# Operand addresses modulo 64 in the dense products, the timing of residual rows, and the buffers of the closing steps of a streaming-encoder block

## The chip, the cores and the metric

The kernel runs on one core of one Trainium2 chip. The time is the device time of one execution in microseconds (us), from launch to end. The profile and the trace come from one further execution of the same program, whose own time and whose span (first to last instruction) are given below.

The engines are named as in the profile: PE is the matrix engine (TensorE) and PEld its loading of the stationary operand, DVE the vector engine, ACT the scalar engine, POOL GpSimd, and SP the engine that issues most DMAs. SPq, ACTq and POOL rows of kind DMA_DIRECT2D are DMA issues on those engines' queues.

## The reference, cut to what matters

One layer over 2048 rows of 1024 numbers, all float32:

```python
h = rms_norm(x, pre_mix_g);  proj = h @ w_in          # 1024 x 5376
y_a = chunk_band_attention(...);  y_b = rwkv7_time_mix(...)
merged = gate_a * (y_a @ proj_a) + gate_b * (y_b @ proj_b)
x = x + rms_norm(merged @ w_out, post_mix_g)
hf = rms_norm(x, pre_ffn_g)
u = square(relu(hf @ w_up)) @ w_down                  # 1024 x 4096, 4096 x 1024
x = x + rms_norm(u, post_ffn_g)
```

## The kernel before

**Dense products.** Each float32 product is made of three fp32r matmuls: every operand is split into a high part (a cast on ACT, line 76) and a low part (a subtraction on DVE, line 77), and `mm3` (line 85) multiplies high by high, high by low and low by high. In the profile a matmul is named out<-moving,stationary: `ps_u<-t3h,s3l` streams 512 columns of `t3h` past a 128 x 128 block of `s3l`.

**Stages.** The 2048 rows are four groups of 512. For each group the *mixing* runs: `w_in` (psd), time mixing, attention, gates (ps_p) and `w_out` (ps_o). Then come the two *halves* of the feed-forward part, two groups each: `phase_up` (tile `ps_u`) and `phase_down` (tile `ps_dn`). Both use Strassen's scheme: seven block products in place of eight. In `phase_up`, block column i (of 16) needs the products A11, A12 (moving operands `bh`, `bl`), S2, S3, S1, S4 and A22 (moving `t2`, `t3`, `t1`, `b22`, `t4`), 12 matmuls each. The products A11 and A12 of the first eight columns are made ahead, and A11 is kept in tile `z`. In `phase_down` a `product` is 4 row tiles of 12 matmuls, seven products for each of three batches, with plain products of four blocks of `w_down` ahead of and behind them.

**Where tiles lie.** Pools grow from both ends of the on-chip memory. On the left stand `const` (ident 512 bytes a partition, g2c 32, nhalf 32), then in mixing the pools of weights and `h`, and in the feed-forward part `z` (which `phase_down` uses for its stationary tiles `fop`), the first half's `b` tiles (`bh`, `bl`, and `fop2` in `phase_down`), and the tiles t1 to t4, b22 and y. On the right stand, in mixing, `mconst` (with `carry`) and the time mixing's tiles, and in the feed-forward part the raw weights, the stationary tiles of `phase_up` (a1, s12, s3, s4), and the second half's `b` tiles.

**Residual rows.** The sums x + rms_norm(merged @ w_out) of groups 2 and 3 (eight row tiles of 128) are made inside the first half's `phase_up`, by the generator `residuals` (line 1070 on). Each `advance(beside, 1)` between two block products runs it to its next `yield`. A row tile takes seven steps: load o and x; squares of o; scale, add and store x1; squares of x; scaled copy (line 1102); two steps of four transposes (line 1110), copies with the gain (line 1112) and a store. Its o and x live in slices 2, 3 and 4, 5 of `z`, and the gain in slices 0, 1. From column HELD = 6 on, each of the last five block products is followed by a step, and from column 8 on the first two share one more.

**Closing steps.** `phase_down` ends with eight row tiles of two halves (n = 0, 1) of 512 columns: the last matmuls are added to y (line 1373), `halve` squares y on ACT (line 1436) and multiplies y by the gain in place on DVE (line 1437), and `final` sums the squares and makes the root on POOL (lines 1443, 130, 132), then multiplies and adds x on DVE (line 1448) and stores from y (line 1449): on POOL's queue in the first half, on SP's and ACT's in the second. `final` of a row tile stands behind the first addition of the next one. Its x row (`x1r`, two buffers) is loaded inside `final`.

**Order.** A tile scheduler orders each engine's instructions from the code's order and its dependencies; `issue_after(ins)` keeps instructions behind `ins` on the same engine. Each engine and each DMA queue runs in that order.

Of the kernel before, what the change touches and what calls it, by code (L numbers as in the profile page):

```python
# [17 lines left out]
P = 128  # L18
# [14 lines left out]
FIRST, BATCHES, XB = 2, 3, 4  # L33
HELD = 6
PARTS = ("a11", "a12", "a22", "s1", "s2", "s3", "s4")
# [18 lines left out]
class Block:  # L54
# [102 lines left out]
    def constants(self, ctx, mixing):  # L157
# [5 lines left out]
        make_identity(nc, self.ident)  # L163
        self.g2c = keep.tile([P, KB], F32, name="g2c")
        self.nhalf = keep.tile([P, 8], F32, name="nhalf")
# [30 lines left out]

        self.carry = cp.tile([P, 14], F32, name="carry")
        nc.vector.memset(self.carry, 0.0)
# [874 lines left out]
    def residuals(self, z, mp, cb, pt):  # L1073
# [13 lines left out]
        for g in range(2, self.NG):  # L1087
            for t in range(GT):
                ts = slice(t * P, (t + 1) * P)
                nc.sync.dma_start(o, self.od[g][t])  # L1090
                nc.sync.dma_start(x, a["x"][g * G + t * P : g * G + (t + 1) * P])
                yield
                r = lengths(o, 0.25 / D, 0.5)
                yield
                with tc.issue_after(self.add):
                    nc.vector.scalar_tensor_tensor(o, o, r, gp, op0=ALU.mult, op1=ALU.mult)
                    nc.vector.tensor_tensor(x, x, o, ALU.add)
                nc.gpsimd.dma_start(self.x1[g][ts], x)
                yield
                r = lengths(x, 1.0 / D, None)  # L1100
                yield
                nc.scalar.activation(o, x, AF.Copy, scale=r)
                yield
                for h in range(2):
                    ps = pt.tile([P, 4, P], F32, tag="tr", name="ps_ht")
                    f = cb.tile([P, 4, P], F32, tag="c", name="hf")
                    with tc.issue_after(self.mm):
                        for j in range(4):
                            k = h * 4 + j
                            nc.tensor.transpose(ps[:, j], o[:, k * P : (k + 1) * P], self.ident)  # L1110
# [81 lines left out]
    def phase_up(self, half, zp, rp, cb, pn, sp, early, made, beside_of=None):  # L1192
# [7 lines left out]
        with ExitStack() as ctx:  # L1200
# [40 lines left out]
            def hidden(src, x, fb, th, out=None):  # L1241
# [4 lines left out]
                self.add = nc.vector.tensor_tensor(out, src, x, ALU.add).ins  # L1246
                nc.scalar.activation(out, out, AF.Relu)
                nc.scalar.activation(out, out, AF.Square)
# [23 lines left out]
            for i in range(FF // P // 2):  # L1272
# [18 lines left out]
                if i < early:  # L1291
                    p1 = z[:, i]
                    if summed(i):
                        nc.sync.dma_start(R["a11"], place(i, "a11"))
                else:
                    p1 = up.tile([P, G], F32, tag="p1", name="p1")
                    nc.scalar.copy(p1, product(A11, B11, self.pd, "d"))
                    hidden(p1, product(A12, B21, self.pd, "d"), 2 * i, 0, out.get("a11"))
                    advance(beside, 1)
# [17 lines left out]
    def phase_down(self, half, zp, bp, rp, cb, pn, follow=None):  # L1317
# [12 lines left out]
        with ExitStack() as ctx:  # L1330
# [100 lines left out]

            def halve(th, t, n, gt, ssq):
# [3 lines left out]
                nc.scalar.activation(sq, u, AF.Square, accum_out=ssq[:, n : n + 1])  # L1436
                nc.vector.tensor_tensor(u, u, gt[:, ns], ALU.mult)  # L1437

            def final(th, t, fp, ssq):
# [3 lines left out]
                nc.gpsimd.tensor_tensor(ssq[:, 0:1], ssq[:, 0:1], ssq[:, 1:2], ALU.add)  # L1443
# [53 lines left out]
            for th in range(2):  # L1497
                for t in range(GT):
                    ssq = fp.tile([P, 2], F32, tag="ssq", bufs=4, name="ssqu")
                    for n in range(2):  # L1500
# [12 lines left out]
                        halve(th, t, n, gt, ssq)  # L1513
                    done = th, t, fp, ssq
            final(*done)
# [3 lines left out]
    def run(self):  # L1519
        tc, e = self.tc, None  # L1520
        with ExitStack() as ctx, ExitStack() as mixing:
# [47 lines left out]
            with ExitStack() as c:  # L1569
                bp = bpool(c, "b")  # L1570
                advance(self.first_half(0, bp))
                with self.nc.allow_non_contiguous_dma(reason="one vector"):
                    self.nc.gpsimd.dma_start(self.g2c, self.a["pre_ffn_g"].rearrange("(k p) -> p k", p=P))
                with ExitStack() as u:
# [53 lines left out]
```

## Time and profile before

| | us |
|---|---|
| median of three runs (lowest, highest) | 3335.2 (3334.75, 3336.52) |
| the profiled execution | 3334.86 |
| its span | 3333.2 |
| mixing (four groups), 0 to 2021.3 of the span | 2021.3 |
| first half up / down, to 2359.3 / 2679.5 | 338.0 / 320.2 |
| second half up / down, to 2998.8 / 3333.2 | 319.3 / 334.4 |

The stages are cut at the first matmul of each. A row of the timeline gives start, busy time, engine, line, operation, tiles and count; in brackets the engine's idle time before it and what ended it. Rows with a count merge instructions that follow each other, so their busy time runs from the first start to the last end. A row of the waits gives who waited for whom, the sum in us, how often, and the longest.

### The profile page before, as it was taken

Reading aid. Unit: us, or ns where it says so; the run is one execution under the profiler, and the core shown is the slowest. Engines: PE = TensorE matmul, PEld = TensorE weight load, DVE = VectorE, ACT = ScalarE, POOL = GpSimd, SP = SyncE. Lnnn points to the kernel's source line nnn. Section 1 sums busy time; section 2 is a strip of 40 time slices with the busy share of each in tenths; the row PEclk is TensorE's granted clock in tenths of the full one; section 3 lists DMA queues with packets and bytes.
Section 4 is the critical chain, followed back from the end, with each engine's and each line's share of the span. In section 5 each row is a group of like instructions: output and inputs, shape, how many; then the busy total and the mean of one; then the engine's idle time right before and its main releaser. Section 6 shows DMA issues by size and latency. Waiting matters only on the chain. (4 is left out here: it accounts for less than half of the span.)

```text
span 3333.2 us, 49202 instructions
## 1 busy us (share of the span) xinstructions
PE 3236.2 (97%) x18945; PEld 2578.1 (77%) x18945; DVE 2271.5 (68%) x3782; ACT 1571.5 (47%) x2551; POOL 386.6 (12%) x757
## 2 busy tenths in 40 slices
PE   7999999999999999999999999999999999999998
PEld 6877787877777877778777777778788877887887
DVE  6784557765566765666775665777678978776687
ACT  4535534445644444645444635466443454454332
POOL 2110011101021011021111000133000111100001
PEclk9999999999999999999999999999999999999999
DMA  5224343225273234273224266566455564543443
GB/s 157 90 89 148 106 143 108 73 93 179 89 244 120 64 105 169 84 240 127 77 96 154 72 230 215 191 235 229 175 189 202 177 225 168 169 164 134 158 151 126
DMA packets 165874, 497.29 MB, mean 149 GB/s; under 512 B 18108, under 2 KB 26496, under 8 KB 160264
## 3 DMA queue, kind: packets, MB, share of 16 engines
q1 hardware_dynamic: 106740, 357.78, 32.5%
q0 software_dynamic: 22688, 77.61, 6.1%
q10 hardware_dynamic: 36212, 58.76, 4.8%
q8 instruction: 149, 2.44, 0.3%
q14 instruction: 85, 0.70, 0.1%
HBM read 365.08 MB, written 132.15 MB: 149 GB/s over the span
## 5 line engine op out<-in xcount | busy, mean ns | idle before, releaser
L85 PE MATMUL psd<-hh,whi 128*128 128x512 f32 x1344 | 542.0, 403 | 6.1 <-ACT whi L76 3.9
L85 PE MATMUL psd<-hl,whi 128*128 128x512 f32 x1344 | 534.8, 398 | 0.4 <-DVE hl L154 0.4
L85 PE MATMUL psd<-hh,wlo 128*128 128x512 f32 x1344 | 535.1, 398 | 0.0
L85 PE MATMUL ps_dn<-fop,fop 128*128 128x512 f32 x2016 | 464.5, 392 | 1.4 <-DVE y L1373 1.0
L76 ACT CAST whi<-wraw 128x1024 fp32r<-128x1024 f32 x232 | 243.3, 1049 | 460.7 <-PE psd L85 326.7
L85 PEld LDWEIGHTS ps_dn<-fop,fop 128*128 128x128 f32 x2016 | 378.2, 188 | 87.4 <-issue 2.1
L77 DVE TENSOR_TENSOR wlo<-wraw,whi 128x1024 fp32r<-128x1024 f32 x232 | 282.8, 1219 | 143.3 <-ACT whi L76 128.4
L85 PEld LDWEIGHTS psd<-hh,whi 128*128 128x128 f32 x1344 | 253.4, 189 | 62.6 <-ACT whi L76 4.6
L85 PEld LDWEIGHTS psd<-hh,wlo 128*128 128x128 f32 x1344 | 253.7, 189 | 56.0 <-issue 3.5
L85 PEld LDWEIGHTS psd<-hl,whi 128*128 128x128 f32 x1344 | 254.2, 189 | 48.9 <-issue 2.2
L76 ACT CAST fop<-ar 128x1024 fp32r<-128x1024 f32 x84 | 87.8, 1050 | 221.6 <-PE ps_dn L85 177.3
L85 PE MATMUL ps_dn<-fop 128*128 128x512 f32 x768 | 178.5, 393 | 1.6 <-DVE y L1373 1.2
L85 PEld LDWEIGHTS ps_dn<-fop 128*128 128x128 f32 x768 | 143.5, 188 | 36.0 <-DVE y L1373 3.1
L1373 DVE TENSOR_TENSOR y<-y,ps_dn 128x512 f32<-128x512 f32 x168 | 110.6, 685 | 50.2 <-PE ps_dn L85 49.9
L77 DVE TENSOR_TENSOR fop<-ar,fop 128x1024 fp32r<-128x1024 f32 x84 | 102.4, 1222 | 44.2 <-ACT fop L76 44.2
L904 DVE CUSTOM_DVE_ANT_0 sc<-bias,ps_s 128x640 f32<-128x640 f32 (+4 forms) x128 | 94.2, 736 | 51.6 <-PE ps_s L898 49.0
L909 ACT ACTIVATE sc<-sc,mn 128x640 f32<-128x640 f32 (+4 forms) x128 | 97.7, 763 | 35.4 <-DVE mn L904 30.9
L1029 PE MATMUL ps_o<-wlo,mh 128*128 128x512 f32 x256 | 103.1, 403 | 5.7 <-DVE wlo L77 5.7
L1029 PE MATMUL ps_o<-whi,ml 128*128 128x512 f32 x256 | 102.5, 400 | 0.0
L85 PE MATMUL ps_p<-yh,whi 128*128 128x512 f32 x256 | 101.1, 395 | 1.3 <-DVE th L995 1.3
L85 PE MATMUL ps_p<-yh,wlo 128*128 128x512 f32 x256 | 101.5, 396 | 0.2 <-DVE wlo L77 0.2
L1029 PE MATMUL ps_o<-whi,mh 128*128 128x512 f32 x256 | 101.6, 400 | 0.0
(384 smaller groups left out, 6819.2 us busy)
## 6 DMA issues: line engine op xcount, KB each, us to landing
wraw<-in_w_in_dram SPq DMA_DIRECT2D x168, 512.0 KB, 3.7
ar<-sd SPq DMA_DIRECT2D x42, 1024.0 KB, 4.6
wraw<-in_w_up_dram SPq DMA_DIRECT2D x80, 512.0 KB, 4.9
sd<-slots POOLq DMA_DIRECT2D x96, 256.0 KB, 5.2
qb<-in_w_down_dram SPq DMA_DIRECT2D x24, 1024.0 KB, 7.5
gd<-gate ACTq DMA_DIRECT2D x64, 256.0 KB, 3.4
wraw<-in_w_out_dram SPq DMA_DIRECT2D x32, 512.0 KB, 3.7
sd<-slots ACTq DMA_DIRECT2D x60, 256.0 KB, 4.5
```

The source lines that it names most:

```text
L76: self.nc.scalar.copy(hi, src)
L77: self.nc.vector.tensor_tensor(lo, src, hi.bitcast(F32), ALU.subtract)
L85: mm = nc.tensor.matmul(ps, l, r, start=start and n == 0, stop=stop and n == last).ins
L904: nc.vector.tensor_tensor_reduce(sc[:, 0:n], bias[:, s0:640], pss[:, c0 : c0 + n], 1.0, 3.0e38, ALU.add, ALU.min, mn,)
L909: nc.scalar.activation(sc[:, 0:n], sc[:, 0:n], AF.Exp, scale=-1.0, bias=mn, accum_out=sm)
L1029: nc.tensor.matmul(ps[t], l[:, k, ts], r[:, k % 2], start=k == 0 and j == 0, stop=k == KB - 1 and j == 2)
L1373: self.add = nc.vector.tensor_tensor(dst, dst, ps, ALU.add).ins
```

## The change

The change has three parts. No instruction is added or removed on PE, DVE, ACT, POOL or a DMA queue; waits, places and addresses change.

1. **Addresses.** g2c is allocated with 64 bytes instead of 32 and carry with 88 instead of 56, so everything behind g2c on the left, and everything inside of carry on the right during mixing, moves by 32 bytes. Start addresses modulo 64 in the built program:

| product | moving, stationary before | after |
|---|---|---|
| psd, ps_p, ps_o (mixing) | 0, 0 | 32, 32 |
| ps_u with t1 to t4, b22 (both halves) | 0, 32 | 32, 32 |
| ps_u with bh, bl: first half / second half | 0, 32 / 32, 32 | 32, 32 / 32, 32 |
| ps_dn, seven products: first half / second half | 0, 0 / 32, 0 | 32, 32 / 32, 32 |
| ident with left tiles / with the time mixing's tiles (transposes) | 0, 0 / 0, 32 | 0, 32 / 0, 0 |
| small products of the time mixing's low-rank weights (64 matmuls) | 32, 32 | 0, 32 |

2. **Residual rows.** HELD is 5; a row tile takes nine steps: o is loaded a step ahead of x, and a step is put between the scaled copy and the transposes. Squares and copy stand behind the latest relu of the products on ACT (`self.act`). Column 5 gets steps, and columns from 8 on get one more.
3. **Closing steps.** The product with the gain goes to a new tile `scaled` (two buffers); x has four buffers, is loaded at the start of its row tile's step, takes the sum, and is stored from.

```diff
-HELD = 6
+HELD = 5
-        self.g2c = keep.tile([P, KB], F32, name="g2c")
+        self.g2c = keep.tile([P, 2 * KB], F32, name="g2c")
-        self.carry = cp.tile([P, 14], F32, name="carry")
+        self.carry = cp.tile([P, 22], F32, name="carry")
...
                 nc.sync.dma_start(o, self.od[g][t])
+                yield
                 nc.sync.dma_start(x, a["x"][g * G + t * P : g * G + (t + 1) * P])
                 yield
-                r = lengths(o, 0.25 / D, 0.5)
+                with tc.issue_after(self.act):
+                    r = lengths(o, 0.25 / D, 0.5)
...
-                r = lengths(x, 1.0 / D, None)
+                with tc.issue_after(self.act):
+                    r = lengths(x, 1.0 / D, None)
                 yield
-                nc.scalar.activation(o, x, AF.Copy, scale=r)
+                with tc.issue_after(self.act):
+                    nc.scalar.activation(o, x, AF.Copy, scale=r)
+                yield
                 yield
...
-                nc.scalar.activation(out, out, AF.Relu)
+                self.act = nc.scalar.activation(out, out, AF.Relu).ins
...
                     nc.scalar.copy(p1, product(A11, B11, self.pd, "d"))
+                    advance(beside, 1)
                     hidden(p1, product(A12, B21, self.pd, "d"), 2 * i, 0, out.get("a11"))
...
-                nc.vector.tensor_tensor(u, u, gt[:, ns], ALU.mult)
+                nc.vector.tensor_tensor(scaled[:, ns], u, gt[:, ns], ALU.mult)
...
-                x = fp.tile([P, D], F32, tag="x", name="x1r")
-                nc.sync.dma_start(x, self.x1[gs[th]][t * P : (t + 1) * P])
...
-                    u = y[th][:, t, ns]
-                    nc.vector.scalar_tensor_tensor(u, u, r, x[:, ns], op0=ALU.mult, op1=ALU.add)
-                    queue.dma_start(self.out[row : row + P, ns], u)
+                    nc.vector.scalar_tensor_tensor(
+                        x[:, ns], scaled[:, ns], r, x[:, ns], op0=ALU.mult, op1=ALU.add
+                    )
+                    queue.dma_start(self.out[row : row + P, ns], x[:, ns])
...
                 for t in range(GT):
+                    scaled = fp.tile([P, D], F32, tag="scaled", name="scaled")
+                    x = fp.tile([P, D], F32, tag="x", bufs=4, name="x1r")
+                    nc.sync.dma_start(x, self.x1[gs[th]][t * P : (t + 1) * P])
```

What the change moves is shown at two places. The first is SP, from the closing steps of the first half to the start of the second half's `phase_up`: x1r are the x rows, wraw the raw weights of `phase_up`, bl and t2l operands of the second half. Before:

```order
L1171 DMA bl<-ht_338 128x1024 x3
L1442 DMA x1r<-x_0_316 128x1024
L1178 DMA wraw<-in_w_up_dram 128x1024 x3
L1442 DMA x1r<-x_0_316 128x1024
L1178 DMA wraw<-in_w_up_dram 128x1024
L1442 DMA x1r<-x_1_317 128x1024 x4
L1178 DMA wraw<-in_w_up_dram 128x1024 x2
L1219 DMA t2l<-td_373 128x1024 x2
L1219 DMA t3l<-td_373 128x1024 x2
```

The same place on SP after the change:

```order
L1506 DMA x1r<-x_1_317 128x1024
L1176 DMA bl<-ht_338 128x1024
L1183 DMA wraw<-in_w_up_dram 128x1024 x2
L1506 DMA x1r<-x_1_317 128x1024
L1183 DMA wraw<-in_w_up_dram 128x1024 x2
L1506 DMA x1r<-x_1_317 128x1024 x2
L1183 DMA wraw<-in_w_up_dram 128x1024
L1224 DMA t2l<-td_373 128x1024 x2
L1224 DMA t3l<-td_373 128x1024 x2
```

One load of raw weights instead of two now stands between the last x row and t2l, and the four loads of x rows in a row are spread.

The second place is DVE in the second half's closing steps, one row tile and the start of the next. Before:

```order
L1448 SCALAR_TENSOR_TENSOR y_26897<-y_26897,rs_r,x1r 128x512 x2
L1437 TENSOR_TENSOR y_26898<-y_26898,g_post_28785 128x512
L1373 TENSOR_TENSOR y_26898<-y_26898,ps_dn 128x512
L1437 TENSOR_TENSOR y_26898<-y_26898,g_post_28785 128x512
L1373 TENSOR_TENSOR y_26898<-y_26898,ps_dn 128x512
```

The same place on DVE after the change:

```order
L1451 SCALAR_TENSOR_TENSOR x1r<-scaled,rs_r,x1r 128x512 x2
L1443 TENSOR_TENSOR scaled<-y_26906,g_post_28793 128x512
L1379 TENSOR_TENSOR y_26906<-y_26906,ps_dn 128x512
L1443 TENSOR_TENSOR scaled<-y_26906,g_post_28793 128x512
L1379 TENSOR_TENSOR y_26906<-y_26906,ps_dn 128x512
```

The order is the same; the product with the gain no longer overwrites what ACT squares, so it no longer waits for ACT.

More of the change, by code (lines that the diff above doesn't have):

```diff
@@ L1430, in add, with halve @@
                 nc.vector.tensor_tensor(o[:, t], o[:, t], x[:, t], ALU.add)
-            def halve(th, t, n, gt, ssq):
+            def halve(th, t, n, gt, scaled, ssq):
                 ns = slice(n * H, (n + 1) * H)
@@ L1436, in halve, with final @@
                 nc.scalar.activation(sq, u, AF.Square, accum_out=ssq[:, n : n + 1])
-                nc.vector.tensor_tensor(u, u, gt[:, ns], ALU.mult)
-            def final(th, t, fp, ssq):
+                nc.vector.tensor_tensor(scaled[:, ns], u, gt[:, ns], ALU.mult)
+            def final(th, t, fp, scaled, x, ssq):
                 row = gs[th] * G + t * P
-                x = fp.tile([P, D], F32, tag="x", name="x1r")
-                nc.sync.dma_start(x, self.x1[gs[th]][t * P : (t + 1) * P])
                 nc.gpsimd.tensor_tensor(ssq[:, 0:1], ssq[:, 0:1], ssq[:, 1:2], ALU.add)
@@ L1512, in phase_down @@
                             advance(beside, 1)
-                        halve(th, t, n, gt, ssq)
-                    done = th, t, fp, ssq
+                        halve(th, t, n, gt, scaled, ssq)
+                    done = th, t, fp, scaled, x, ssq
             final(*done)
@@ L1572, in run @@
                 with self.nc.allow_non_contiguous_dma(reason="one vector"):
-                    self.nc.gpsimd.dma_start(self.g2c, self.a["pre_ffn_g"].rearrange("(k p) -> p k", p=P))
+                    self.nc.gpsimd.dma_start(self.g2c[:, 0:KB], self.a["pre_ffn_g"].rearrange("(k p) -> p k", p=P))
                 with ExitStack() as u:
```

## The prediction

> **What bounds the kernel.** I read the page first, then the stages cut at their first matmul, then the starts of PE's matmuls in the timeline.
>
> ```profile
> span 3333.2 us, 49202 instructions
> PE 3236.2 (97%) x18945; PEld 2578.1 (77%) x18945; DVE 2271.5 (68%) x3782; ACT 1571.5 (47%) x2551; POOL 386.6 (12%) x757
> ```
>
> PE is busy for 97%. So there are two ways to gain: its matmuls come closer together, or the few waits between them go. The stages, with the busy time (count) of PE, PEld, DVE, ACT and POOL, the granted clock, the DMA share and GB/s; first the mixing, then first half up and down, second half up and down, and last a stretch ahead of the final closing steps:
>
> ```profile
> 0.00:2021.30 2021.30, 1953.94 (x13410) 1543.98 (x13411) 1292.04 (x2545) 964.17 (x1649) 253.13 (x513) 0.99 0.38 128
> 2021.30:2359.30 338.00, 327.11 (x1410) 260.73 (x1409) 240.99 (x318) 201.65 (x359) 69.20 (x128) 0.98 0.63 219
> 2359.30:2679.50 320.20, 317.64 (x1394) 260.78 (x1393) 258.80 (x312) 124.88 (x161) 20.91 (x34) 1.00 0.53 186
> 2679.50:2998.80 319.30, 313.02 (x1346) 252.06 (x1345) 231.45 (x312) 160.13 (x226) 31.89 (x58) 1.00 0.52 181
> 2998.80:3333.20 334.40, 324.47 (x1393) 260.52 (x1391) 248.20 (x297) 120.66 (x160) 11.46 (x24) 0.99 0.41 143
> 3257.00:3288.00 31.00, 31.00 (x135) 24.88 (x134) 28.95 (x38) 11.74 (x12) 0.00 (x0) 1.00 0.29 102
> ```
>
> The two halves do the same products with different times, and in opposite ways: up takes 338.0 and 319.3 us, down 320.2 and 334.4. The count of matmuls is nearly the same and the clock is 1.00 in two of the four, 0.98 and 0.99 in the others. The timeline of PE (start, busy time, line, tiles, count) shows more:
>
> ```profile
> 2404.29 75.87 PE L85 MATMUL ps_dn<-fop,fop 128*128 128x512 f32 x334
> 3099.74 80.43 PE L85 MATMUL ps_dn<-fop,fop 128*128 128x512 f32 x344
> ...
> 2026.87 0.40 PE L85 MATMUL ps_u<-bh,s12h 128*128 128x512 f32 x1
> ...
> 2032.47 0.40 PE L85 MATMUL ps_u<-bh,s3h 128*128 128x512 f32 x1
> ...
> 2843.01 0.40 PE L85 MATMUL ps_u<-bh,a1h 128*128 128x512 f32 x1
> ...
> 2848.46 0.40 PE L85 MATMUL ps_u<-t2h,s12h 128*128 128x512 f32 x1
> ...
> 2851.26 0.40 PE L85 MATMUL ps_u<-t3h,s3h 128*128 128x512 f32 x1
> ```
>
> The last matmul of a run is busy for about 0.4 us, so starts lie (75.87 − 0.39)/333 = 226.7 ns apart in the first half's down stage, where both operands start at 0 modulo 64, and (80.43 − 0.40)/343 = 233.3 ns in the second half's, where they are at 32 and 0. In up it is the reverse: 24 starts from bh,s12h at 2026.87 to bh,s3h at 2032.47 (0 and 32) are 233.3 ns each; 24 from 2843.01 to 2848.46 in the second half (32 and 32) are 227.1; and the 12 that follow at once, with t2 (0 and 32), are 233.3 again. The price follows the agreement of the two addresses through one stretch of one stage, and not the stage or the clock.
>
> **Part 1, addresses.** How many matmuls change from disagreeing to agreeing:
>
> ```profile
> L85 PE MATMUL ps_u<-t3h,s3l 128*128 128x512 f32 x128 | 52.1, 407 | 3.4 <-DVE s3l L77 3.4
> L85 PE MATMUL ps_u<-bh,a1h 128*128 128x512 f32 x176 | 69.5, 395 | 2.8 <-ACT z L1267 2.8
> L85 PE MATMUL ps_u<-bh,s12h 128*128 128x512 f32 x48 | 19.1, 397 | 1.8 <-ACT z L1267 1.5 <-DVE r L1246 0.3
> L85 PE MATMUL ps_u<-bh,s3h 128*128 128x512 f32 x32 | 12.6, 392 | 0.0
> L85 PE MATMUL ps_dn<-fop,fop 128*128 128x512 f32 x2016 | 464.5, 392 | 1.4 <-DVE y L1373 1.0 <-DVE v L1373 0.3
> L916 PE MATMUL ps_pt<-ident,sc 128*128 128x128 f32 x560 | 85.5, 279 | 2.0 <-ACT VV L857 1.2 <-DVE sc L912 0.8
> L516 PE MATMUL ps_bk<-ident,BK 128*128 128x128 f32 x128 | 21.6, 281 | 0.0
> ```
>
> Five products with t1 to t4 and b22, three matmul groups of 128 each: 1920, in both halves. The products with bh and bl, 3 × (176 + 48 + 32) = 768, of which the first half's 384 change. Of the 2016 in down, the second half's 1008. Together 3312. Between the rows above the difference is 233.3 − 227.1 = 6.2 ns or 233.3 − 226.7 = 6.6. At 6.2, which is from neighbouring products of one stage, that is 20.5 us (at 6.6 21.9): 8.3 in the first half's up (1344), 6.0 in the second's (960), 6.2 in the second's down.
>
> Three deductions. The 64 small products that lose their agreement cost 64 × 6.2 ns = 0.4. In the 31 us ahead of the last closing steps DVE is busy for 28.95, 93%, so PE cannot run ahead of it: its 135 matmuls give back 0.8. And where PE waits for a split (the row of s3l below), a faster PE waits longer; two columns of 84 matmuls so lose 2 × 84 × 6.2 ns = 1.0. **A = 20.5 − 2.2 = 18.3 us.** The 5568 matmuls of psd, ps_p and ps_o go from 0, 0 to 32, 32 and still agree: nothing. If it were the 0 that counts they would be dear; that is a rival below. The transposes I put at nothing: those of sc agree with ident before and take 279 ns, those of BK don't and take 281. The largest group, 560, loses its agreement: between nothing and 560 × 2 ns = 1.1 us, which the 128 of BK give back in part.
>
> One rule of the Trainium skill speaks against this term. Its page "TensorE: Matmul & The Clock Gate", section "Step-by-step: what each phase is for", says that PE has two independent SBUF read ports and that loading the next weights "doesn't steal SBUF read bandwidth from the running matmul". By it A would be nothing and the sum 3320; the rows at 2843 to 2851 disagree with it, 227.1 against 233.3 ns.
>
> **Part 2, residual rows.** The waits of the columns with residual rows, 2170 to 2360 (who waited for whom: sum, times, longest), one row tile in the timeline, and the granted clock behind the longest of these waits:
>
> ```profile
> PEld ps_ht L1110 <- ACT z L1102: 8.2, 5, 2.6
> PE ps_ht L1110 <- ACT z L1102: 5.6, 4, 1.9
> PEld ps_u L85 <- DVE s3l L77: 2.2, 1, 2.2
> ...
> 2193.98 0.63 ACT L1082 ACTIVATE sqo<-z 128x512 f32<-128x512 f32 x1 [0.70 <-DVE z L1097]
> ...
> 2198.12 0.63 ACT L1247 ACTIVATE slots<-slots 128x512 f32<-128x512 f32 x1 [2.80 <-DVE slots L1246]
> ...
> 2200.03 1.15 ACT L1102 ACTIVATE z<-z,rs_r 128x1024 f32<-128x1024 f32 x1 [0.61 <-POOL rs_r L132]
> 2201.24 1.09 PE L1110 MATMUL ps_ht<-ident,z 128*128 128x128 f32 x8 [1.09 <-ACT z L1102]
> ...
> 2348.00:2353.00 5.00, 4.35 (x16) 3.65 (x17) 2.36 (x2) 4.46 (x8) 0.85 (x1) 0.66 0.60 222
> ```
>
> The row tile's squares, relu, copy and transposes stand in the middle. From the squares of x (2193.98) to the end of the scaled copy (2201.18) it takes 7.2 us; the code gives it two steps of 12 matmuls, 2 × 2.8 = 5.6, so PE arrives first and waits. With the additional step it has three, 36 × 0.227 = 8.2, and the wait goes with 1.0 to spare. PE lost between 5.6 (its own row) and 8.2 us (that of PEld, under which the previous matmul still runs), middle 6.9. The clock behind the longest wait is 0.66 for 5 us, so its 4.35 busy us would have taken (at 1.00) about 4.35 × 0.66 = 2.9: 1.5 more. **B = 6.9 + 1.5 = 8.4.**
>
> What it adds: column 5 gets steps, DVE work of a row tile that lay elsewhere before, and the order "behind the relu" on ACT. In the row at 2198.12 the relu itself comes 2.80 late from DVE; squares that stand behind such a relu start up to 2.8 late, and behind them POOL's sum and the copy. Over 1.0 spare that leaves at most 1.8 for a row tile. The next waits are on s3l (2.2) and on the transposes' results. B lies between 3 and 11 (8.2 + 1.5, and half of s3l's wait if the spread of steps frees DVE).
>
> **Part 3, closing steps.** The end of the second half:
>
> ```profile
> 3290.64 0.19 POOL L1443 TENSOR_TENSOR ssqu<-ssqu 128x1 f32<-128x1 f32 x1 [324.88 <-ACT squ L1436]
> ...
> 3308.67 15.03 PE L85 MATMUL ps_dn<-fop 128*128 128x512 f32 x64
> ...
> 3319.96 0.68 DVE L1373 TENSOR_TENSOR y<-y,ps_dn 128x512 f32<-128x512 f32 x1
> ...
> 3321.49 0.69 DVE L1437 TENSOR_TENSOR y<-y,g_post 128x512 f32<-128x512 f32 x1 [0.85 <-ACT squ L1436]
> 3321.54 0.70 POOL L1443 TENSOR_TENSOR ssqu<-ssqu 128x1 f32<-128x1 f32 x1 [3.54 <-ACT squ L1436]
> ...
> 3325.11 0.68 DVE L1373 TENSOR_TENSOR y<-y,ps_dn 128x512 f32<-128x512 f32 x1
> ```
>
> PE ends at 3323.70, but the last sum on DVE starts at 3325.11, 1.4 us later. DVE's chain over a row tile has a period of 3325.11 − 3319.96 = 5.15, and in it the product with the gain (line 1437) waits 0.85 for ACT's squares and then starts together with POOL's sum, which takes 0.70 in its company and 0.19 alone (the row at 3290.64). With its own output tile the product starts behind the addition; POOL's sum is then 0.5 shorter and the period about 4.65, under PE's 24 × 0.227 = 5.45. So DVE keeps up and the lag of 1.4 goes, as do 0.5 from the final chain: **C1 = 1.9** (0.5 to 2). If the product met another POOL instruction instead, 0.5 would stay. The x rows and stores cost nothing here: four buffers of x come round after 4 × 5.15 = 20.6 us.
>
> Between the halves, in the waits of 2680 to 2735 and the timeline of SP and ACT:
>
> ```profile
> PEld ps_u L85 <- ACT z L1267: 5.2, 2, 3.2
> ...
> 2681.16 10.23 SPq L1178 DMA_DIRECT2D wraw<-in_w_up_dram  x2
> 2691.69 0.87 SPq L1219 DMA_DIRECT2D t2l<-td  x2
> ...
> 2697.09 1.05 ACT L1162 CAST t2h<-t2l 128x1024 fp32r<-128x1024 f32 x1 [1.99 <-DMA t2l<-td]
> ```
>
> The first products of the second half wait 5.2 us for copies on ACT (z), which stand behind the closing steps' squares and the cast of t2. t2l comes late: its load is issued at 2691.69, behind two loads of raw weights that held SP's queue for 10.23, and its memory is that of y, which the stores of the closing steps still read. After the change one load of weights stands ahead of it, stores read x, and DVE's chain is shorter by the 0.85 and 0.5 of above. The waits could go whole (5.2, with some 1.5 more ahead of them) or stay whole, if t2l's load is held by its data's own late write. I take **C2 = 4.5** (0 to 6.7), nearer to the upper end since both of its causes are moved.
>
> **Sum.** 18.3 + 8.4 + 1.9 + 4.5 = 33.1 us. Against the profiled execution, 3334.86 − 33.1 = 3301.8; the median of the runs, 3335.2, is 0.3 above it. Forecast 3302, chance 0.80; its own range from the terms' ends is 3295 (A 21.9 − 2.2, B 11, C 2 + 6.7) to 3313 (A 18.3, B 3, C 0.5).
>
> **Rivals.** *DVE and ACT pace the up stages* (0.11). DVE is busy for 241 of 338.0 us in the first half's up, 71%, ACT for 60%, and the load is uneven. If half of the 14.3 us of both up stages is given back in longer waits for splits (7), and half of B (4), the time is 3302 + 11 = 3313. Against it: PE's idle time in these stages is only 11 and 6 us.
>
> *The change of addresses does nothing* (0.05): the 6.6 ns belong to something else that changes from half to half. In every disagreeing pair of these rows one tile lies on the left and one on the right, so "the other end of the memory" would explain the rows as well. Then A is 0: 3301.8 + 18.3 = 3320. Against it: by the addresses of the built program, in the first half t1 lies at 144 to 158 KB and s12 at 181 to 185, close by, and its starts are 233 ns apart; in the second half b lies at 169 to 199 KB and a1 at 141 to 145, as far, with 227. If B and C came to less than 8 of their 14.8 as well, the time would be within 0.2% of before.
>
> *Slower: the 0 counts, and not the agreement* (0.04). If a tile at 32 costs the price whatever the other is, the mixing's 5568 matmuls go from free to dear: 5568 × 6.6 ns = 36.7, and A is 0: 3320 + 37 = 3357. It decides against the change from 14.8/5568 = 2.7 ns a matmul on. Against it stands the row pair at 2843.01 and 2848.46: 32 and 32, 227.1 ns.
>
> **Chances and range.** About 0.2%, 6.7 us, is what a measurement of this kernel can tell from no change. Faster by more: forecast 0.80, DVE and ACT 0.11, and 0.02 of "nothing", 0.93; within: 0.03; slower: 0.04. The range 3294 to 3316 holds the forecast's own range, a microsecond for the transposes at its lower end, and the first rival, whose share beyond 3313 reaches some 3 further.
>
> **What would show it.** Starts 227 ns apart in all four stages of the halves, and mixing still 2021 us long (2058 by the slower rival). No wait of ps_ht on z over 1 us, and no clock of 0.66 behind it. POOL's sum at 0.19 in the closing steps, and the last addition within 0.3 us of PE's last matmul. The wait on z at the second half's start below 2 us, with t2l's load issued some 5 us sooner behind PE's first matmul of the stage or ahead of it. Wrong would be: 233 ns anywhere in the halves, or waits for splits in the up stages that grow by more than 3 us together.

## The result, and the profile after

The changed kernel takes 3311.0 us (median of four runs, 3308.97 to 3313.13) against 3335.0 before. The ratio is 0.9932 with a 95% interval of 0.9915 to 0.9949: it is faster by 22.7 us (17 to 28). A second set of runs, beside other kernels, gave 0.9935 (0.9922 to 0.9948). The forecast was 3302 and the range 3294 to 3316. So the direction and the size are right, and about 10 us of the forecast 33 are missing. By stage, in the profiled executions:

| stage | before | after | forecast for the stage | measured |
|---|---|---|---|---|
| mixing | 2021.3 | 2016.3 | 0 | −5.0 |
| first half up | 338.0 | 326.0 | −16.7 (addresses 8.3, residual rows 8.4) | −12.0 |
| first half down | 320.2 | 330.3 | 0 | +10.1 |
| second half up | 319.3 | 313.1 | −10.5 (addresses 6.0, start 4.5) | −6.2 |
| second half down | 334.4 | 325.7 | −8.1 (addresses 6.2, end 1.9) | −8.7 |

The forecasts by stage are those of the terms before the small deductions. Of the mixing's 5 us some 0.8 belong to the change: 384 of the products ps_p go from 229.1 to 226.9 ns, as shown below. The rest is open. Three profiles with the mixing of before have 2018.1 to 2021.3 us, mean 2020.1, and eight with the changed one 2013.5 to 2019.7, mean 2016.3, so that the two overlap. The first row to look at is the third: a stage in which nothing was to happen is 10 us longer. These are the windows of the changed kernel, with the columns as before:

```profile
0.00:2016.30 2016.30, 1950.36 (x13410) 1541.11 (x13411) 1292.07 (x2545) 964.89 (x1649) 252.32 (x513) 1.00 0.38 128
2016.30:2342.30 326.00, 315.80 (x1409) 258.99 (x1408) 239.94 (x317) 195.95 (x347) 65.73 (x126) 0.99 0.65 227
2342.30:2672.60 330.30, 320.08 (x1396) 262.55 (x1395) 258.62 (x310) 129.65 (x171) 17.72 (x35) 0.99 0.51 182
2672.60:2985.70 313.10, 307.76 (x1346) 253.01 (x1345) 231.54 (x315) 159.29 (x226) 31.62 (x60) 0.99 0.53 183
2985.70:3311.40 325.70, 317.19 (x1393) 260.67 (x1391) 247.91 (x297) 121.18 (x160) 7.62 (x24) 0.99 0.41 146
```

In the first half's down stage (third row) the granted clock is 0.99 where it was 1.00, and ACT does 129.65 us of work where it did 124.88: five us of ACT's work came over from the stage before. The timeline of PE and one group of matmuls show the addresses:

```profile
2403.69 26.68 PE L85 MATMUL ps_dn<-fop,fop 128*128 128x512 f32 x117
...
3098.73 41.64 PE L85 MATMUL ps_dn<-fop,fop 128*128 128x512 f32 x183
...
L85 PE MATMUL ps_u<-t3h,s3l 128*128 128x512 f32 x128 | 50.1, 391 | 1.9 <-DVE s3l L77 1.9
```

In the second half's down stage starts are now (41.64 − 0.39)/182 = 226.6 ns apart, as in the first half's ((26.68 − 0.39)/116 = 226.6); before they were 233.3. The mean of t3h,s3l fell from 407 to 391 ns.

Next, the waits of the columns with residual rows (2130 to 2342 us), and ACT, PE and the windows at the seam of the first half's two stages:

```profile
PEld ps_ht L1115 <- ACT z L1106: 8.3, 5, 2.1
PE ps_ht L1115 <- ACT z L1106: 6.1, 5, 1.7
...
2341.45 1.09 PE L1115 MATMUL ps_ht<-ident,z 128*128 128x128 f32 x8 [1.66 <-ACT z L1106]
...
2345.83 0.63 ACT L1117 ACTIVATE hf<-ps_ht,g2c 128x128 f32<-128x128 f32 x2
2350.89 1.14 ACT L1117 ACTIVATE hf<-ps_ht,g2c 128x128 f32<-128x128 f32 x4 [4.43 <-DMA ad<-r]
2351.90 1.58 ACT L1377 COPY y<-ps_dn 128x512 f32<-128x512 f32 x3
...
2352.56 6.68 PE L85 MATMUL ps_dn<-fop 128*128 128x512 f32 x18 [7.26 <-ACT y L1377]
...
2352.00:2358.00 6.00, 5.44 (x14) 4.29 (x15) 0.00 (x0) 4.34 (x9) 0.75 (x1) 0.54 1.04 413
```

Read from below: PE stands still for 7.26 us at the start of down, waiting for ACT's copies of the first sums (y<-ps_dn), and then runs at a granted clock of 0.54. ACT is late with these copies because it stands at 2346.5 to 2350.9 in front of the last four copies with the gain (hf). These want a buffer which they share with the tiles r, and by the profile the store of such a tile (ad<-r, issued on ACT's queue between 2341.9 and 2345.5) is still under way. The last row tile's eight transposes (2341.45) are now the last work of the up stage. Before, its two groups of four stood 10.6 and 6.0 us ahead of the first matmul of down:

```profile
2348.65 1.11 PE L1110 MATMUL ps_ht<-ident,z 128*128 128x128 f32 x4 [1.92 <-ACT z L1102]
...
2353.21 0.60 PE L1110 MATMUL ps_ht<-ident,z 128*128 128x128 f32 x4
...
2359.24 1.09 PE L85 MATMUL ps_dn<-fop 128*128 128x512 f32 x4
```

And the waits of transposes on the scaled copy, which were to go, are as before: 8.3 us (PEld) and 6.1 (PE) against 8.2 and 5.6.

At the start of the second half, the waits of PE in the first 55 us and SP's load of t2l:

```profile
PEld ps_u L85 <- ACT z L1272: 2.8, 1, 2.8
...
2675.38 0.91 SPq L1224 DMA_DIRECT2D t2l<-td  x2
2679.29 0.63 ACT L1442 ACTIVATE squ<-y 128x512 f32<-128x512 f32 x1 [2.00 <-DVE y L1379]
```

One wait of 2.8 is left of two with 5.2 together. t2l is loaded 2.8 us behind the stage's first matmul and no longer 12.2. The closing steps of the second half:

```profile
3289.80 13.99 PE L85 MATMUL ps_dn<-fop 128*128 128x512 f32 x61
...
3303.82 0.69 DVE L1379 TENSOR_TENSOR y<-y,ps_dn 128x512 f32<-128x512 f32 x1
3304.54 0.69 DVE L1443 TENSOR_TENSOR scaled<-y,g_post 128x512 f32<-128x512 f32 x1
3305.40 0.19 POOL L1447 TENSOR_TENSOR ssqu<-ssqu 128x1 f32<-128x1 f32 x1 [4.33 <-ACT squ L1442]
```

PE ends at 3303.79 and the last sum starts at 3303.82, where it was 1.4 us late. The product with the gain no longer waits, and POOL's sum takes 0.19.

### The profile page after: what moved, and what is told of

Read it like the earlier page. It is cut to its first block, busy times and chain, and to the rows that moved or that the text cites. A ratio compares the mean times of both kernels' runs of the same rounds, so it can differ in the third digit from the quotient of the medians.

```text
span 3311.4 us, 49181 instructions
## 1 busy us (share of the span) xinstructions
PE 3211.2 (97%) x18945; PEld 2576.3 (78%) x18945; DVE 2270.1 (69%) x3782; ACT 1571.0 (47%) x2551; POOL 375.0 (11%) x757
## 5 line engine op out<-in xcount | busy, mean ns | idle before, releaser
L85 PE MATMUL ps_dn<-fop,fop 128*128 128x512 f32 x2016 | 457.8, 389 | 1.7 <-DVE y L1379 1.3
```

Source lines behind the costliest of these rows:

```text
L85: mm = nc.tensor.matmul(ps, l, r, start=start and n == 0, stop=stop and n == last).ins
```

## The experiments

Each kernel was timed beside the kernel before on the same chip. Runs of one kernel spread widely (the 23 runs of the kernel before in the first set lie between 3326.0 and 3342.0), so ratios are given with intervals, and the stages of a profile say where a difference lies.

| run | ratio (95% interval) | us against before |
|---|---|---|
| e1 addresses | 0.9958 (0.9942 to 0.9974) | −14.0 |
| e2 residual rows | 1.0004 (0.9994 to 1.0014) | +1.3 |
| e3 closing steps | 0.9989 (0.9977 to 1.0001) | −3.7 |
| e4 changed, last tile shorter | 0.9926 (0.9910 to 0.9941) | −24.7 |
| e5 changed kernel again | 0.9935 (0.9922 to 0.9948) | −21.7 |
| e6 changed, without residual rows | 0.9938 (0.9922 to 0.9954) | −20.7 |
| e7 as e4, without the order on ACT | 0.9924 (0.9909 to 0.9939) | −25.3 |
| e8 addresses, g2c alone | 0.9950 (0.9937 to 0.9964) | −16.7 |
| e9 changed, pairs 64 apart | 0.9971 (0.9961 to 0.9981) | −9.7 |
| e10 changed, three steps won back | 0.9908 (0.9896 to 0.9921) | −30.7 |
| e11 changed, gain in place | 0.9964 (0.9951 to 0.9977) | −12.0 |
| e12 as e10, pairs 128 apart | 0.9962 (0.9949 to 0.9976) | −12.7 |

**The three parts alone.** e1 has the allocations of g2c and carry, e2 the residual rows, e3 the closing steps of the diff; each leaves out the other two parts.

> The kernel of before with the addresses alone (part 1). Theory 1 (agreement modulo 64 is worth about 6.3 ns for each of 3312 matmuls, and the 10 us that the first down stage of the changed kernel gained in length come from part 2): 3335 - 20 = 3315 us, starts 227 ns apart in all four stages, first down stage about 320 us as before. Rival (PE reaches the end of the first up stage earlier, and the wait there comes from that): about 3325, with a wait of PE of about 7 us at the start of the first down stage.

> The kernel of before with the residual rows alone (part 2). Theory 1 (there is one step fewer than the nine steps of eight row tiles need, so the last row tile's transposes and its copies with the gain come at the very end of the up stage, ahead of ACT's copies of the first down sums): slower than before, 3335 + 10 - 4 = 3341, with a wait of about 7 us on ACT's copies at the start of the first down stage and starts of 427 ns behind it. Rival (the wait needs the faster PE of part 1 as well): 3331 to 3335, without that wait.

> The kernel of before with the closing steps alone (part 3). Theory 1 (it takes about 2 us from the last stage; at the start of the second half one wait goes and another grows): 3332 to 3333, POOL's sum at 0.19 us. Rival (term C2 as predicted, hidden in the changed kernel by its other parts): 3328 to 3329, with the waits on z at the second half's start below 2 us together.

e1: starts are 227 ns apart in all four stages of the halves, as theory 1 has it, but the ratio is worth 14.0 us (8.7 to 19.3), and theory 1's 20 lies just outside. The profiled execution, the slowest of the six, shows where a part can stay: PE's waits at the seam to the first down stage and in front of its products were 2.8 and 2.9 us, where they were 0.3 and 1.0 before, with thirteen starts of 427 ns behind the second. The first down stage was 326.6 and not 320. So in this execution a piece of the rival holds as well: a PE that arrives sooner waits longer for engines that have not become faster. It is not so in each: in e8, which has the same pairs in the halves, the wait at the seam is 0.4 us and the stage 320.8.

e2: the time doesn't move, +1.3 us (−2.0 to +4.7). The up stage is 8.7 us shorter (329.3) and the down stage 8.6 longer (328.9). The waits of PE in the first 50 us of that down stage:

```profile
PEld ps_dn L85 <- ACT y L1377: 6.8, 1, 6.8
PE ps_dn L85 <- ACT y L1377: 6.4, 1, 6.4
```

The same wait as in the changed kernel, without the faster PE: it belongs to the residual rows. Theory 1 was right on the wait, and its sum, which gave the up stage only 4 us, was about 5 too high.

e3: 3.7 us (0.3 slower to 7.7 faster), between the two theories. In its profile the wait of 3 us for z behind t2's cast is gone, the wait ahead of it grew from 1.6 to 2.1 us with seven starts of 427 ns behind it, and the last stage is 1.4 us shorter.

**Where the last row tile stands.** Eight row tiles of nine steps are 72. Columns 5 to 7 give five steps each and columns 8 to 15 seven each, 71 in all; what is left runs behind the last product. Before, 56 steps were wanted and 58 given. e4 takes two steps away from the last row tile:

```diff
                 nc.sync.dma_start(o, self.od[g][t])
-                yield
+                final = g == self.NG - 1 and t == GT - 1
+                if not final:
+                    yield
...
                 yield
-                yield
+                if not final:
+                    yield
```

> The changed kernel, whose last row tile alone goes without the added load step and the added empty step, so that its transposes stand two products earlier. Theory 1: the wait of 7 us and the slow starts behind it go, the first down stage is back at about 320 us: 3311 - 10 + 1 = 3302. Rival (the wait is that of the down stage's own operands or loads and not of the residual rows): 3311, and the first down stage still about 330.

The first down stage is back at 320.5 us, and the wait of 7 us is gone, as theory 1 has it. But the last tile's transposes then wait 3.6 us for their scaled copy, and the up stage is 328.0 where it was 326.0. By the times alone, 0.9926 against 0.9932 and 0.9935, e4 can't be told from the changed kernel.

e10 wins three steps back without shortening the last tile: the first load of all starts at the end of column 4, and the fourth and fifth tile, whose scaled copies were ready 2.6 and 2.0 us ahead of their transposes, do without the empty step.

```diff
                 yield
-                yield
+                if (g, t) not in ((2, 3), (3, 0)):
+                    yield
...
-                advance(beside, steps)
+                advance(beside, 1 if i == HELD - 1 else steps)
```

> The changed kernel with three steps won back for the last row tile, which keeps its nine: the first load starts one step sooner, in column 4, and two row tiles that had over 2 us to spare (the fourth and fifth) go without the empty step. Theory 1: the last transposes stand three products earlier, the 10 us at the start of the first down stage go and the up stage stays as in the changed kernel, ratio 0.9905 to 0.991. Rival (the work at the end of the up stage is too much for ACT wherever the last tile stands): another wait of 3 us or more at the end of up or the start of down, ratio 0.9925 or above.

0.9908, where 0.9905 to 0.991 was expected; its interval ends below both values of the changed kernel, though the intervals overlap. The two stages in its windows, and the waits of the transposes from 2130 us on:

```profile
2016.90:2337.90 321.00, 314.03 (x1409) 257.94 (x1408) 241.48 (x318) 201.34 (x359) 66.92 (x128) 1.00 0.67 229
2337.90:2660.10 322.20, 318.39 (x1394) 260.47 (x1394) 255.98 (x310) 125.02 (x160) 16.17 (x33) 1.00 0.53 188
...
PEld ps_ht L1116 <- ACT z L1106: 6.0, 5, 1.5
PE ps_ht L1116 <- ACT z L1106: 3.8, 4, 1.1
```

Up is 321.0 and down 322.2, with the clock at 1.00 in both: 13.1 us less than the changed kernel in the two stages. The up stage, which was to stay as it was, is itself 5.0 shorter than in the changed kernel's first profile and 2.9 shorter than in its second (e5). This is the fastest kernel of the study, 30.7 us (26 to 35) ahead of the one before.

**The part as a whole, and the order on ACT.** e6 is the changed kernel with the residual rows of before; e7 is e4 without the three `issue_after(self.act)`.

> The kernel of before with parts 1 and 3, without the residual rows. Theory 1 (part 2 gives back at the start of the first down stage what it brings in the up stage, as alone): ratio as that of the changed kernel within 0.1%, no wait of 7 us at the start of the first down stage, and waits of the transposes on the scaled copy of 7 to 9 us together in the up stage. Rival (with part 1 in place part 2 brings its 8 us): ratio 0.0025 higher than that of the changed kernel.

> The changed kernel with the last row tile mended as in the run before, and without the order behind the relu on ACT for squares and scaled copies. Theory 2 (that order starts the squares some 2 us later and so eats the added step): the four waits of 1.25 us of transposes on the scaled copy go, ratio 0.990 to 0.991. Rival (the chain is late for DVE's sums and POOL's queue, wherever ACT's squares stand): these waits stay, ratio as with the last tile mended, 0.9926.

e6 takes as long as the changed kernel (0.9938 and 0.9935), with a first down stage of 320.4 us and an up stage of 334.2: in the change as it was made, the residual rows bring nothing. e7 does not settle its question. The four waits (1.1 us each on PE in e4) are gone, as theory 2 says, but there are two new ones of 1.7 and 2.9 us, that of the last tile is 2.0, and the time is that of e4.

**What the addresses have to agree in.** e8 was to shift the left side by 16 bytes:

```diff
-        self.g2c = keep.tile([P, KB], F32, name="g2c")
+        self.g2c = keep.tile([P, KB + 4], F32, name="g2c")
```

> The kernel of before with everything behind g2c on the left moved by 16 bytes and not by 32: the pairs that stood at 0 and 32 stand at 16 and 32, the mixing's pairs at 16 and 16. Theory 1 (what counts is whether the two start addresses agree modulo 64): starts 233 ns apart where they were before and 227 in the mixing, time as before, ratio 1.000. Rival (the price goes with the distance of the two): 230 ns, ratio 0.997. Rival (addresses have to be multiples of 32): 233 ns and more everywhere, ratio above 1.008.

In the built program the tiles behind g2c stand 32 bytes further and not 16, so this run is part 1 without carry, and says nothing on the rivals named. As that it is a repetition of e1: 16.7 us (12 to 21). What it lacks shows in the products ps_p with a right tile: their starts are 233.4 ns apart, where they were 229.1 before and are 226.9 in the changed kernel (means over 370 steady starts of each trace).

In e9 the left side moves by another 64 bytes (g2c with 4 * KB), in e12 by another 128 (6 * KB, on e10). The residues modulo 64 are the same as in the changed kernel, 32 and 32.

> The changed kernel with everything behind g2c on the left moved by another 64 bytes: the pairs that stood 32 bytes apart before the change now stand 64 apart modulo 128 (32 and 96), and agree modulo 64. Theory 1 (agreement modulo 64 is what counts): starts 227 ns apart in all stages, ratio as the changed kernel, 0.9935. Rival (the two addresses have to agree modulo 128 or more): 233 ns where they were before, ratio 0.998 to 0.999.

> The kernel with the steps for the last row tile (e10), whose left side moves by another 128 bytes, so that the pairs in question stand 128 apart modulo 256 (352 and 480 modulo 512), where they are 0 apart in the changed kernel (224 and 480). In the run with 64 apart their starts were 229 and 233 ns apart, so agreement modulo 64 is not enough. Theory 3a (agreement modulo 128 is enough): 227 ns everywhere, ratio as e10, 0.991. Theory 3b (they have to agree modulo 256): 229 ns or more for ps_u and ps_dn of the second half, ratio 0.993 to 0.996.

Theory 1 falls with e9, whose starts are not 227 ns apart and which keeps only 9.7 of some 22 us. e12 has the starts of theory 3b; its ratio, 0.9962, is at the upper end of what that expected. Three rows of e9's timeline and, last, one of e12:

```profile
2800.26 0.39 PE L85 MATMUL ps_u<-t3h,s3h 128*128 128x512 f32 x1
...
2803.01 0.39 PE L85 MATMUL ps_u<-t1h,s12h 128*128 128x512 f32 x1
...
3099.70 30.49 PE L85 MATMUL ps_dn<-fop,fop 128*128 128x512 f32 x130
...
3109.64 30.61 PE L85 MATMUL ps_dn<-fop,fop 128*128 128x512 f32 x131
```

Twelve starts of t3 take 2.75 us in e9, 229.2 ns each; in down they are (30.49 − 0.40)/129 = 233.3 ns apart, the full price of before, with the same residues modulo 64. In e12 it is (30.61 − 0.40)/130 = 232.4. The means over all steady starts of the traces follow, by how far the moving address lies ahead of the stationary one modulo 256. The addresses are those of the built programs.

| distance modulo 256 | where | mean of starts, ns |
|---|---|---|
| 0 | changed kernel, up and down of both halves (480 and 224 modulo 512 among them); ps_o of the fourth group | 226.7 to 227.2 |
| 32 | before, second half down; e8, ps_p | 233.3; 233.4 |
| 64 | e9 up; ps_p before | 229.0; 229.1 |
| 128 | e12 up, t tiles; ps_o of the first three groups, before and changed | 232.8; 232.8 and 232.5 |
| 192 | e9 second half down; e9, ps_p | 233.3; 233.3 |
| 224 | before, up | 233.3 |

So agreement modulo 256 is enough, and agreement modulo 64 or 128 is not. In the changed kernel all pairs of the two halves agree modulo 256; that is what brings the gain there. I overlooked one group: the 576 products ps_o (`w_out`) of the first three groups stand 128 apart, before and after the change. Two rows of the changed kernel, 24 starts apart:

```profile
451.43 0.40 PE L1029 MATMUL ps_o<-whi,mh 128*128 128x512 f32 x1
...
457.02 0.39 PE L1029 MATMUL ps_o<-whi,mh 128*128 128x512 f32 x1
```

These starts are 232.9 ns apart, while the same products of the fourth group, 0 apart in both kernels, take 227.2. Bringing the 576 to agree would be worth about 3 us (576 × 5.3 ns), an estimate from these rows that no run tried.

**The gain in place.** e11 is the changed kernel in which the product with the gain overwrites y again:

```diff
-                nc.vector.tensor_tensor(scaled[:, ns], u, gt[:, ns], ALU.mult)
+                nc.vector.tensor_tensor(u, u, gt[:, ns], ALU.mult)
```

> The changed kernel with the product with the gain written in place into y again; x still takes the sum and is stored. Theory 1 (in place the product waits for ACT's squares and then meets POOL's sum): POOL's sum 0.70 us again, the last sum on DVE 1.4 us or more behind PE's end, last stage 1.9 us longer. Rival (the gain of the last stage comes from the x rows and their stores): POOL's sum 0.19, last stage as in the changed kernel.

```profile
3289.81 7.19 PE L85 MATMUL ps_dn<-fop 128*128 128x512 f32 x31
...
3299.23 0.68 DVE L1379 TENSOR_TENSOR y<-y,ps_dn 128x512 f32<-128x512 f32 x1
3300.76 0.69 DVE L1443 TENSOR_TENSOR y<-y,g_post 128x512 f32<-128x512 f32 x1 [0.85 <-ACT squ L1442]
3300.80 0.70 POOL L1447 TENSOR_TENSOR ssqu<-ssqu 128x1 f32<-128x1 f32 x1 [3.54 <-ACT squ L1442]
...
2667.34 10.22 SPq L1183 DMA_DIRECT2D wraw<-in_w_up_dram  x2
2677.61 0.96 SPq L1224 DMA_DIRECT2D t2l<-td  x2
...
ACT t2h L1167 <- DMA t2l<-td: 3.2, 1, 3.2
```

Theory 1 holds: POOL's sum takes 0.70 again, the last sum starts 2.2 us behind PE's end (3297.00), and the last stage is 327.7 us, 2.0 longer than in the changed kernel. The last three rows, from SP and the waits at the start of the second half, were not expected: with stores from x and four buffers, but y read until the end, two loads of weights again stand ahead of t2l and hold SP's queue for 10.22 us, t2l's load is issued 12.0 us behind the stage's first matmul (2665.62), and t2 waits for it as before. The times differ by 10 us from the changed kernel; the stages of the one profile explain 3 of them, and the rest stays open.

## Why the prediction came out as it did

**Addresses (A, 18.3).** The number of matmuls and their price were right: 233.3 to between 226.7 and 227.2 ns, 6.1 to 6.6 each, in all three stages. The two measurements of the part alone give 14.0 (8.7 to 19.3) and 16.7 (12 to 21); 18.3 lies within both, above their middles. In the profiles of e1 and e8 the second half's down stage gains 6.4 and 6.5 us, as forecast (6.2), and the two up stages together 7.9 and 14.2 of 14.3. So in one of the two profiles 6 us were given back there, about what the first rival names (7): in e1 the waits of the transposes grew to 9.4 (PEld) and 7.3 us (PE), from 8.2 and 5.6, and the clock of the first up stage stayed at 0.98, where e8 has 1.00. But the reason was wrong in its number: the sum holds because the 32 bytes bring the pairs of the halves together modulo 256 as well, and that was luck; the shifts of e9 and e12 agree modulo 64 too and lose most of it. All disagreeing pairs of the profile before differ by 32 modulo 64, and from this I took modulo 64; the two pairs I weighed could not tell it from modulo 256. Rows that could were in the trace before: the ps_p products at 0 and 192 took 229.1 ns and the ps_o products at 192 and 64 took 232.8, and not 227, though both agree modulo 64. So "still agree" does not hold for these 960 of the mixing's 5568 matmuls, and for the 384 ps_p the change brought 0.8 us where nothing was forecast. The rule of the Trainium skill ("TensorE: Matmul & The Clock Gate", section "Step-by-step: what each phase is for") that weight loads take nothing from the running matmul's reads gave 3320. The runs disagree: with nothing but addresses changed (e1), starts go from 233.3 to 226.7 ns. That the reads of the two operands collide is the obvious reading, since only their distance counts, but no run here shows what happens inside.

**Residual rows (B, 8.4).** This is the step that failed, twice. First, "with the additional step it has three, and the wait goes with 1.0 to spare": the waits are 8.3 and 6.1 us, as before. Without part 2 but with the faster matmuls they are 9.4 and 7.3 (e1) or 10.1 and 8.0 (e6), so the added step brings 1 to 2 us of the 6.9. I counted the chain from the squares of x in one row tile and took it that it would start at its step. In the changed kernel it starts late, as the timeline of one row tile shows:

```profile
2197.93 0.62 ACT L1082 ACTIVATE sqo<-z 128x512 f32<-128x512 f32 x1
...
2201.69 1.28 DVE L1098 SCALAR_TENSOR_TENSOR z<-z,rs_p 128x1024 f32<-128x1024 f32 x1 [1.32 <-POOL rs_p L135]
2202.89 1.22 DVE L77 TENSOR_TENSOR s3l<-wraw,s3h 128x1024 fp32r<-128x1024 f32 x1
2204.03 1.22 DVE L1099 TENSOR_TENSOR z<-z 128x1024 f32<-128x1024 f32 x1
2205.28 0.63 ACT L1082 ACTIVATE sqo<-z 128x512 f32<-128x512 f32 x1 [2.90 <-DVE z L1099]
...
2206.14 1.75 POOL L1265 DMA_DIRECT2D sd<-slots  x3
2207.91 0.96 POOL L1083 TENSOR_TENSOR ssqo<-ssqo 128x1 f32<-128x1 f32 x1
2209.23 0.57 POOL L132 TENSOR_TENSOR rs_r<-rs_v,nhalf 128x1 f32<-128x1 f32 x1
2209.83 1.15 ACT L1106 ACTIVATE z<-z,rs_r 128x1024 f32<-128x1024 f32 x1 [0.85 <-POOL rs_r L132]
2211.03 0.66 PE L1115 MATMUL ps_ht<-ident,z 128*128 128x128 f32 x4 [1.14 <-ACT z L1106]
```

Three steps ahead of the transposes, 8.2 us before PE is ready at 2209.9, would be 2201.7. The squares of x start at 2205.28: ACT had been waiting 2.90 us for the sum on DVE, which itself ended at 2205.25. In this row it is not the relu that holds them. DVE had idled 1.32 us for the root of the squares of o (2197.93), which POOL makes, and had put the split of s3 (1.22) between the product and the sum. POOL then issues three DMAs (1.75) ahead of its sum, begins it 1.4 us behind the squares and takes 0.96 for it. So the added step went into a chain that was late ahead of it: from the squares of o to the end of the scaled copy it takes 13.05 us, for which five steps give 5 × 2.72 = 13.6, but it starts 1.7 late, at 2197.93 instead of 2196.3. The squares of o stand behind a relu, as part 2 orders them; how much that order adds in each tile was not settled (e7). Second, I listed what column 5 and ACT's order add, but did not count the steps against the places, 72 against 71. The last tile's copies so came between the last stores of the up stage and ACT's first copies of the down stage, and cost 10 us there (7.3 of waiting, 2 at half the clock). Alone the part costs 1.3 us (2.0 faster to 4.7 slower) where −8.4 was forecast, which is below the 3 that the prediction gave as its lower end. e2 has the wait without the faster matmuls, e6 has neither the residual rows nor the wait, and e10, with three steps more, is 8 to 9 us faster than the changed kernel: the loss at the seam is this. Mended in that way the part is worth about 10 us (0.9908 against e6's 0.9938).

**End of the second half (C1, 1.9).** Right in each number: POOL's sum 0.19 for 0.70, no lag of the last sum, last stage 2.0 us longer when the product goes back in place. In the profiles of all kernels whose pairs agree it is 324.7 to 325.7 us with the closing steps as in the change, and 328.0 and 327.9 without them (e1, e8).

**Start of the second half (C2, 4.5).** Half right. The wait for t2l goes, in e3 as in the changed kernel, and with it the loads of weights that held SP's queue: one load, 0.33 us, now stands ahead of t2l. e11 tells which part of the change does this. It has the stores from x and the four buffers, and yet two loads of weights ahead of t2l and a wait of 3.2 us. So the stores that I named are not enough; it takes the new tile, with which y is read last by the product with the gain and no longer by the final sum. Why the loads are then ordered otherwise was not followed. The other wait, for the copy of z behind the last squares, did not shrink but went from 1.6 to 2.4 us, because DVE's last sum of the closing steps starts 5.9 us behind the first matmul of the new stage where it was 5.2, and seven starts of 427 ns came with it. In this one profile about nothing is left of 4.5 beside the addresses' 6.0. Over the profiles of all kernels whose pairs agree the stage takes 311.1 to 313.6 us with the closing steps as in the change and 315.5 and 313.8 without (e1, e8), so the term is some 2 us.

Of the 33.1 forecast 22.7 came. B, which brought between −1.3 (e2) and +1 us (the changed kernel against e6), accounts for 7 to 10 of the missing 10. A and the closing steps came out 2 to 4 and 3 us short where they were measured alone (3.7 against 6.4), each within its interval. The parts alone add up to 16 to 19 us, less than the whole; the intervals leave room for that, and no run explains it. That the time lies within the range although B fell below its lower end is therefore in part luck: the range was wide enough for A and C to carry it.

**The rivals.** The time, 3311, lies nearer to the first rival's 3313 than to the forecast's 3302, but not for its reason: PE's waits for splits in the two up stages, which were to grow by more than 3 us, are 7.0 us together where they were 6.8, and what is missing lies in B. "The 0 counts" is out: at 32 and 32 the mixing is no longer than before. "The change of addresses does nothing" is out as well, and with it the side of the memory, since left and right tiles that agree modulo 256 cost nothing.

## What to carry to other kernels

Operand addresses can be worth 3% of a stream of matmuls, at the price of a few bytes of padding; compare the starts of like matmuls between stages, and test an explanation by a shift that it says is harmless before building on it. Where side work is spread over steps of a loop, count the steps against the places: what is left over lands at the seam, in front of the next stage's first work. And a faster engine at the bound moves the seams first: look there for waits that grew.

## What the runs showed of the hardware

- Matmuls of 512 columns whose moving and stationary address agree modulo 256 had starts 226.7 to 227.2 ns apart. With the moving address 64 ahead it was 229.0, and with 32, 128, 192 and 224 it was 232.4 to 233.4. Other distances were not tried.
- A stall of PE can cost more than its length: behind 7.3 us came ten starts of 427 ns in place of 227, 2 us more. Behind waits of 1.8 to 2.9 us there were none in some places (2.9 in e5, 2.8 in e8) and several in others (seven behind 1.8 and 2.4 in the changed kernel, thirteen behind 2.9 in e1). The Trainium skill ("TensorE: Matmul & The Clock Gate", section "Part 1: The HAM clock gate") describes a clock of half speed after an idle window that runs freely; the granted clock of 0.54 and the 427 ns agree with it, and so does the chance in it. The window it gives is about 3.4 us; here such starts came also behind a wait of 1.8 us, which is shorter.
- Executions of one program on one core spread by 16 us (3326.0 to 3342.0 in 23 runs); the three runs shown ahead of the change spread by 1.8. The 0.2% that the prediction took for a measurement's limit is about right for the ratios here, whose intervals reach 0.10 to 0.17% to each side, and not for single runs.
